# The state space's parameters of a hybrid trunk, moved from VectorE to GpSimd

## The chip, the core and the metric

The kernel runs on one core of a Trainium2 chip. Its engines are TensorE (PE, the matmuls; PEld is its weight load), VectorE (DVE), ScalarE (ACT), GpSimd (POOL) and SyncE (SP, which issues the DMAs here). Each engine works through its own instructions in a fixed order; semaphores hold an instruction back until its inputs are there. The metric is the device time of one execution in microseconds (us), less being better.

## What is computed

Two layers over a sequence of 256 positions with 2048 channels. The first ("even") layer projects its input by one wide matrix and feeds a state-space mixer and a gated MLP; the second ("odd") is a differential attention. The change touches only the mixer's parameters, which are small: 64 groups of 64 complex states, 4096 numbers, held as 128 partitions x 32.

```python
def s5_mixer(u, lam_re, lam_im, log_dt, b_re, b_im, c_re, c_im, d_skip):
    dt = jnp.exp(log_dt.astype(f32))[:, None]
    mag = jnp.exp(lr * dt)
    ab_re = mag * jnp.cos(li * dt)
    ab_im = mag * jnp.sin(li * dt)
    den = lr * lr + li * li
    nr = ab_re - 1.0
    f_re = (nr * lr + ab_im * li) / den
    f_im = (ab_im * lr - nr * li) / den
    ...
    _, _, h_re, h_im = lax.associative_scan(combine, (a_re, a_im, bu_re, bu_im), axis=1)
```

The kernel replaces the scan over positions by matmuls with tables of powers of the complex factor `ab`, and computes exp, sine and cosine itself from polynomials.

## The kernel before

**Weights.** The time goes into matmuls with fp32 weights that are streamed from memory in chunks of four 128-row tiles (two halves of 128x1024 each). Every weight is split in two: ACT makes a rounded copy `wh`, and DVE subtracts it to get the rest, `wl` (one DVE instruction of 128x1024 per half chunk, line 61). PE then makes three passes: `wh` by the high part of the activations (`hh`), `wl` by `hh`, and `wh` by their low part (`hl`). There are three buffers each for `wr` (raw), `wh` and `wl`, so DVE can be at most three half chunks ahead of PE. The activations' own low part `hl` is made by DVE in the first 25 us.

**Order of the chunks.** The first layer's projection runs as `v` (chunks 0 to 7), `xa` (8 to 15), `u` (16 to 23), then the gates, the output projection, and the odd layer. `xa` feeds the mixer, `u` and `v` the gated MLP. A chunk of `xa` is 48 matmuls. The main products share one PSUM pool of two buffers, so the first matmul of `u` needs the buffer that the first half of `xa` fills; it is free when DVE has read it out (`xs <- xa,rbc`).

**Side work.** Three generators run beside these matmuls. `ssm_params()` (line 386) computes, on arrays of 128x32, `dt` and `mag` (by `exact_exp`, line 358), sine and cosine (`ph`, `ph_s`, `ph_c`), `ab`, the reciprocal `den`, the factors `fc` and `fa`, and seven repeated squarings `pw[0]` to `pw[6]`. `e_tables(0)` (line 556) builds the table `E` from them: a copy of `pw[0]` into column 1 (line 563), then six steps k = 1 to 6, each of which multiplies the columns so far by `pw[k]` (eight products `em`, four sums into `E`) and so doubles the table. `ssm_consts()` (line 490) clears the blocks `bbr`, `cA`, `cN` on GpSimd, and builds the tables `m1fc`, `m2fc`, `m1fa`, `m2fa`, `m1ab`, `m2ab` on DVE, which ACT copies into `bbr` and `cA`; PE multiplies these (`pk`, 64 small matmuls, lines 532 and 533) and transposes them (`pbt`). GpSimd also scales an identity into `intra` (16 instructions of 128x128, line 482) and masks `bw` (line 657).

**What sets the order.** Each engine's order (but SP's) is fixed before the program runs, by a scheduler that simulates all engines and gives the earliest ready instruction its place. When one instruction's expected time changes, the order of the others on every engine can change with it.

**The helpers.** `tt`, `ts` and `stt` record two-input operations, operations with scalars, and `(a op s) op b`. Each fixes the engine for its line:

```python
    def tt(o, a, b, op, eng=None):
        (eng or V).tensor_tensor(out=o, in0=a, in1=b, op=op)
    def stt(o, a, s, b, op0, op1):
        V.scalar_tensor_tensor(out=o, in0=a, scalar=s, in1=b, op0=op0, op1=op1)
```

Of the kernel before, what the change touches and what calls it, by code (L numbers as in the profile page):

```python
# [10 lines left out]
F32 = mybir.dt.float32  # L11
# [18 lines left out]
def hybrid_trunk_kernel(ctx: ExitStack, tc: tile.TileContext, xT, xtok, w_in0, w_glu, w_out0,  # L30
                        w_in1, w_out1, pk, bc, lng, wsp, rope, subln, fnorm, out):
    nc = tc.nc
    V, A, PE, G, SP = nc.vector, nc.scalar, nc.tensor, nc.gpsimd, nc.sync
# [6 lines left out]
    sm = ctx.enter_context(tc.tile_pool(name="sm", bufs=1))  # L40
# [16 lines left out]
    def bcast(ap, shape):  # L57
        return ap.to_broadcast(shape)

    def tt(o, a, b, op, eng=None):  # L60
        (eng or V).tensor_tensor(out=o, in0=a, in1=b, op=op)  # L61

    def mul(o, a, b):
        tt(o, a, b, ALU.mult)

    def add(o, a, b):
        tt(o, a, b, ALU.add)

    def sub(o, a, b):
        tt(o, a, b, ALU.subtract)  # L70

    def ts(o, a, s1, op0, s2=None, op1=None):
        if op1 is None:
            V.tensor_scalar(out=o, in0=a, scalar1=s1, scalar2=None, op0=op0)
        else:
            V.tensor_scalar(out=o, in0=a, scalar1=s1, scalar2=s2, op0=op0, op1=op1)

    def stt(o, a, s, b, op0, op1):
        V.scalar_tensor_tensor(out=o, in0=a, scalar=s, in1=b, op0=op0, op1=op1)

    def act(o, i, f, **kw):
        A.activation(out=o, in_=i, func=f, **kw)  # L82
# [1 line left out]
    def rsqrt_mean(name, ss, n, eps, post=None):  # L84
# [6 lines left out]
        def v_y2(y):  # L91
            z = t("rq_z")
            if w == 1:
                stt(z, y, v, y, ALU.mult, ALU.mult)
            else:
                mul(z, y, y)
                mul(z, z, v)
            return z

        v = t("rq_v")  # L100
        ts(v, ss, 1.0 / n, ALU.mult, eps, ALU.add)
        g = t("rq_i", I32)
        ts(g, v.bitcast(I32), 1, ALU.logical_shift_right)
        ts(g, g, -1.0, ALU.mult, 1597463007.0, ALU.add)
        y = g.bitcast(F32)
        r = sm.tile([128, w], F32, name=name, tag=name, bufs=2)
        z = v_y2(y)
        u = t("rq_u")
        ts(u, z, 0.375, ALU.mult, -1.25, ALU.add)
        mul(u, u, z)  # L110
        stt(r, u, 1.875, y, ALU.add, ALU.mult)
        z = v_y2(r)
        c = 1.0 if post is None else post
# [84 lines left out]
    side = deque()  # L198
# [63 lines left out]
    def side1(name, shape, lane=0):  # L262
        return psb.tile(shape, F32, name=name, tag=f"sb{lane}")
# [45 lines left out]
    def h_split(k):  # L309
        hi = hh[k // 8][:, k % 8, :]  # L310
        with hp():
            act(hi, xt[:, k, :], AF.Copy, scale=g0[:, k:k + 1])
            stt(hl[k // 8][:, k % 8, :], xt[:, k, :], g0[:, k:k + 1], hi.bitcast(F32), ALU.mult, ALU.subtract)
# [39 lines left out]
    def tr32(name, shape=(128, 32), dt=F32):  # L353
        return sm.tile(list(shape), dt, name=name, tag=f"tr{shape[1]}{'i' if dt == I32 else ''}",
                       bufs=(7 if dt == F32 else 1) if shape[1] <= 32 else 2)

    def exact_exp(o, x, w=32):
        sh = (128, w)
        xc = tr32("e_x", sh)
        ts(xc, x, -104.0, ALU.max, 90.0, ALU.min)  # L360
        n = tr32("e_n", sh)
        ts(n, xc, 1.4426950408889634, ALU.mult)
        ts(n, n, MAGIC, ALU.add)
        ts(n, n, MAGIC, ALU.subtract)
        r = tr32("e_r", sh)
        stt(r, n, -0.693359375, xc, ALU.mult, ALU.add)
        stt(r, n, 2.12194440054690583e-4, r, ALU.mult, ALU.add)
        p = tr32("e_p", sh)
        ts(p, r, 1.0 / 5040, ALU.mult)
        for c in (1.0 / 720, 1.0 / 120, 1.0 / 24, 1.0 / 6, 0.5, 1.0):  # L370
            stt(p, p, c, r, ALU.add, ALU.mult)
        ts(p, p, 1.0, ALU.add)
        n1 = tr32("e_n1", sh)
        ts(n1, n, 0.5, ALU.mult)
        ts(n1, n1, MAGIC, ALU.add)
        ts(n1, n1, MAGIC, ALU.subtract)
        sub(n, n, n1)
        for part in (n1, n):
            e = tr32("e_i", sh, I32)
            ts(e, part, 127.0, ALU.add, 8388608.0, ALU.mult)  # L380
            mul(p, p, e.bitcast(F32))
        V.tensor_copy(out=o, in_=p)

    cst = {}

    def ssm_params():
        dt_ = p32("dt")
        exact_exp(dt_, log_dt)
        yield
        mag = p32("mag")  # L390
        z = tr32("lrdt")
        mul(z, lam_re, dt_)
        exact_exp(mag, z)
        r2 = p32("r2")
        mul(r2, mag, mag)
# [160 lines left out]
    def e_tables(half):  # L556
        E = big.tile([128, 2, 16, 128], F32, name=f"E{half}", tag="e")
        etab[half] = E
        hs = slice(half * 16, half * 16 + 16)
        pw = cst["pw"]  # L560
        V.memset(E[:, 0, :, 0:1], 1.0)
        V.memset(E[:, 1, :, 0:1], 0.0)
        V.tensor_copy(out=E[:, :, :, 1:2], in_=pw[0][:, :, hs].unsqueeze(3))
        for k in range(1, 7):
            n = 1 << k
            for q in range(2):
                ph = slice(q * 8, q * 8 + 8)
                es = E[:, :, ph, 0:n]
                sh = [128, 8, n]
                m = [t4(f"em{half}{k}{q}{i}", [128, 2, 8, 64])[:, :, :, 0:n] for i in range(2)]  # L570
                for i in range(2):
                    a = pw[k][:, i, half * 16 + q * 8:half * 16 + q * 8 + 8].unsqueeze(2).to_broadcast(sh)
                    for c in range(2):
                        mul(m[i][:, c], es[:, c], a)
                o = slice(n, 2 * n)
                sub(E[:, 0, ph, o], m[0][:, 0], m[1][:, 1])
                add(E[:, 1, ph, o], m[0][:, 1], m[1][:, 0])
            if k >= 4:
                yield
        yield  # L580
# [68 lines left out]
        for s in range(4):  # L649
            yield from ssm_set(half * 4 + s)  # L650

    side.append(ssm_params())
    side.append(e_tables(0))
    side.append(ssm_consts())

# [60 lines left out]
    for n in range(2):  # L716
# [4 lines left out]
        with hp():  # L721
            for t in range(2):
                act(ut[:, t, n * 512:(n + 1) * 512], ps[:, t, :], AF.Gelu_apprx_tanh, scale=rsx[0][:, t:t + 1])
                p = side1(f"s{n}{t}", [128, 4, 128])
# [3 lines left out]
                for g in range(4):  # L728
                    h = n * 4 + g
                    o = ut[:, t, h * 128:(h + 1) * 128]  # L730
                    stt(o, p[:, g, :], bspt[:, h:h + 1], o, ALU.add, ALU.mult)
    yh = {1: (t8(15, "yh1", [128, 8, T], F32R), t8(13, "yl1", [128, 8, T], F32R))}
    for n in range(2):
# [4 lines left out]
        with hp():  # L738
            for t in range(2):
                gt = t2(f"gt{n}{t}", [128, 512])  # L740
                act(gt, ps[:, t, :], AF.Silu, scale=rsx[0][:, t:t + 1])
                o = ut[:, t, n * 512:(n + 1) * 512]
                mul(o, o, gt)
            for c in range(2):
                c0 = n * 4 + 2 * c
                p = side1(f"ybT{c0}", [128, 2, T])
# [290 lines left out]
    for t in range(2):  # L1037
        s = slice(t * 128, (t + 1) * 128)
# [20 lines left out]
        for c in range(3):  # L1059
            o = x1[t][:, c * 512:(c + 1) * 512]  # L1060
# [96 lines left out]
```

## Time and profile before

| | before |
|---|---|
| time, median of 3 runs | 888.02 us (887.10 to 888.34) |
| the profiled execution | 886.45 us, of which its span 884.7 |
| PE busy | 866.4 us, 98% of the span |
| DVE busy | 680.2 us, 77% |
| ACT busy | 456.6 us, 52% |
| POOL busy | 36.8 us, 4%, in 55 instructions |

A reader takes the busy shares first (PE leaves 18 us of its span idle), then the stretches of the first 140 us, where the side work lies, and last the order and the start times of single instructions there. The durations that the trace gives for DVE are a little longer than the distance from one start to the next; where instructions follow each other without a gap, the distance is the cost.

### The profile page before, as it was taken

The page shows a single profiled execution, that of the slowest core. Times are in us where ns is not written, and L with a number is a line of the kernel's source. Part 1 is how long each engine was busy: PE and PEld are TensorE (multiplying, and loading weights), DVE is VectorE, ACT ScalarE, POOL GpSimd, SP SyncE. Part 2 cuts the span into 40 slices and gives each one's busy share as a digit, 9 for nine tenths or more (in the row PEclk, how much of TensorE's full clock was granted, in tenths as well). Part 3 has the DMA queues.
Part 4 walks back from the last instruction along what each step waited for, and adds up shares of the span by engine and source line. Part 5 has one row for each costly group of instructions (what it writes and reads, how often), then busy time and mean ns, then how long its engine had stood idle before and what let it go on. Part 6 is the DMA issues. An engine that isn't in the chain of part 4 may idle for free.

```text
span 884.7 us, 13127 instructions
## 1 busy us (share of the span) xinstructions
PE 866.4 (98%) x5086; PEld 749.2 (85%) x5086; DVE 680.2 (77%) x1267; ACT 456.6 (52%) x639; POOL 36.8 (4%) x55
## 2 busy tenths in 40 slices
PE   8999999999999999999999999999999999999995
PEld 6799978788999789888788888888888888888895
DVE  8999869999988766577876688667867687765773
ACT  7563862455334645565445544555446544554551
POOL 7100000000000100000000000000000000000000
PEclk9999999999999999999999999999999999999998
DMA  8965452234534655555554555555554555555542
GB/s 299 409 223 191 144 190 96 96 112 175 190 104 144 261 181 175 184 190 183 168 190 161 173 191 190 191 159 176 189 191 154 180 190 195 189 187 190 180 154 96
DMA packets 55167, 160.19 MB, mean 181 GB/s; under 512 B 3392, under 2 KB 37440, under 8 KB 41024
## 3 DMA queue, kind: packets, MB, share of 16 engines
q1 hardware_dynamic: 54528, 156.20, 50.4%
q0 software_dynamic: 576, 3.15, 0.9%
q8 instruction: 40, 0.66, 0.3%
q14 instruction: 23, 0.19, 0.1%
HBM read 157.24 MB, written 2.10 MB: 180 GB/s over the span
## 4 chain that ended last, share of the span: by engine, by line
PE 88%; DVE 7%; ACT 2%; issue 1%; DMA 1%; SPq 0%; DVEq 0%; ACTq 0%
PE k L249 7%; PE q L249 7%; PE v L223 4%; PE v L224 4%; PE v L222 4%; PE k L250 3%; PE q L250 3%; PE g L224 3%; PE g L223 3%; PE g L222 3%; PE od L223 2%; PE od L222 2%; PE od L224 2%; PE ga L235 2%; PE ga L238 2%; PE ga L237 2%
## 5 line engine op out<-in xcount | busy, mean ns | idle before, releaser
L82 ACT ACTIVATE wh<-wr 128x1024 fp32r<-128x1024 f32 (+1 forms) x276 | 288.7, 1047 | 347.5 <-PE v L224 59.6
L61 DVE TENSOR_TENSOR wl<-wr,wh 128x1024 fp32r<-128x1024 f32 (+1 forms) x276 | 332.2, 1206 | 131.1 <-ACT wh L82 130.0
L249 PE MATMUL k<-h2p,wh 128*128 128x512 f32 x256 | 90.7, 397 | 1.9 <-DVE rm L61 1.9
L249 PE MATMUL q<-h2p,wh 128*128 128x512 f32 x256 | 90.4, 396 | 0.0
L250 PE MATMUL q<-h2p,wl 128*128 128x256 f32 x256 | 72.3, 283 | 0.1
L250 PE MATMUL k<-h2p,wl 128*128 128x256 f32 x256 | 71.9, 282 | 0.0
L249 PEld LDWEIGHTS k<-h2p,wh 128*128 128x128 f32 x256 | 48.0, 188 | 13.3 <-DVE rm L61 2.2
L249 PEld LDWEIGHTS q<-h2p,wh 128*128 128x128 f32 x256 | 48.0, 188 | 10.8
L223 PE MATMUL v<-wl,h2p 128*128 128x512 f32 x128 | 50.8, 397 | 0.0
L223 PE MATMUL g<-wl,h2p 128*128 128x512 f32 x128 | 50.3, 393 | 0.0
L224 PE MATMUL g<-wh,h2p 128*128 128x512 f32 x128 | 50.1, 391 | 0.0
L224 PE MATMUL v<-wh,h2p 128*128 128x512 f32 x128 | 50.0, 391 | 0.0
L222 PE MATMUL g<-wh,h2p 128*128 128x512 f32 x128 | 49.9, 390 | 0.0
L222 PE MATMUL v<-wh,h2p 128*128 128x512 f32 x128 | 49.9, 390 | 0.0
L250 PEld LDWEIGHTS q<-h2p,wl 128*128 128x128 f32 x256 | 48.3, 189 | 0.6 <-DVE wl L61 0.4
L250 PEld LDWEIGHTS k<-h2p,wl 128*128 128x128 f32 x256 | 48.4, 189 | 0.1
L223 PE MATMUL od<-wl,oh 128*128 128x512 f32 x96 | 37.6, 392 | 0.0
L222 PE MATMUL od<-wh,oh 128*128 128x512 f32 x96 | 37.5, 391 | 0.0
L224 PE MATMUL od<-wh,ol 128*128 128x512 f32 x96 | 37.2, 390 | 0.0
L235 PE MATMUL ga<-hh,wh 128*128 128x256 f32 x128 | 36.6, 286 | 0.0
L238 PE MATMUL ga<-hh,wl 128*128 128x256 f32 x128 | 36.5, 286 | 0.0
L237 PE MATMUL ga<-hl,wh 128*128 128x256 f32 x128 | 36.4, 285 | 0.0
(329 smaller groups left out, 2057.7 us busy)
## 6 DMA issues: line engine op xcount, KB each, us to landing
wr<-in_w_in_dram SPq DMA_DIRECT2D x68, 1024.0 KB, 4.8
wr<-in_w_in_dram SPq DMA_DIRECT2D x68, 512.0 KB, 5.1
wr<-in_w_out_dram SPq DMA_DIRECT2D x32, 1024.0 KB, 4.8
wr<-in_w_glu_dram SPq DMA_DIRECT2D x4, 1024.0 KB, 4.8
wr<-in_w_in_dram SPq DMA_DIRECT2D x8, 256.0 KB, 4.8
xk<-in_xtok_dram SPq DMA_DIRECT2D x2, 1024.0 KB, 10.2
xr<-in_xtok_dram POOLq DMA_DIRECT2D x2, 1024.0 KB, 7.3
out_dram<-x SPq DMA_DIRECT2D x6, 256.0 KB, 2.5
```

The lines of the kernel that those rows point to most:

```text
L61: (eng or V).tensor_tensor(out=o, in0=a, in1=b, op=op)
L82: A.activation(out=o, in_=i, func=f, **kw)
L222: PE.matmul(ps[:, t, :], hi[:, s], wh, start=first and a == 0, stop=False)
L223: PE.matmul(ps[:, t, :], hi[:, s], wl, start=False, stop=False)
L224: PE.matmul(ps[:, t, :], lo[:, s], wh, start=False, stop=last and a == len(ktiles) - 1)
L235: PE.matmul(ps[:, c, :], wh[:, s], hi, start=first and a == 0 and c % 2 == 0, stop=False, skip_group_check=True)
L237: PE.matmul(ps[:, c, :], wh[:, s], lo, start=False, stop=False, skip_group_check=True)
L238: PE.matmul(ps[:, c, :], wl[:, s], hi, start=False, stop=fin, skip_group_check=True)
L249: PE.matmul(ps[:, c, :], wh[:, s], hl, start=first and a == 0, stop=False, skip_group_check=True)
L250: PE.matmul(ps[:, c, T:], wl[:, s], hl[:, 0], start=False, stop=a == len(ktiles) - 1 and not first, skip_group_check=True)
```

## The change

The three helpers no longer name VectorE but look up a list with one entry, `el`. A new wrapper `on_pool` sets the entry to GpSimd while the generator `ssm_params()` takes a step, and back to VectorE after it. [...]

```diff
+    el = [V]
+
     def tt(o, a, b, op, eng=None):
-        (eng or V).tensor_tensor(out=o, in0=a, in1=b, op=op)
+        (eng or el[0]).tensor_tensor(out=o, in0=a, in1=b, op=op)
...
     def stt(o, a, s, b, op0, op1):
-        V.scalar_tensor_tensor(out=o, in0=a, scalar=s, in1=b, op0=op0, op1=op1)
+        if el[0] is G:
+            n = o.shape[-1]
+            z = sm.tile([128, n], F32, name="gz", tag=f"gz{n}", bufs=1)
+            ts(z, a, s, op0)
+            tt(o, z, b, op1)
+        else:
+            V.scalar_tensor_tensor(out=o, in0=a, scalar=s, in1=b, op0=op0, op1=op1)
...
-        V.tensor_copy(out=o, in_=p)
+        el[0].tensor_copy(out=o, in_=p)
...
+    def on_pool(steps):
+
+        while True:
+            el[0] = G
+            try:
+                next(steps)
+            except StopIteration:
+                return
+            finally:
+                el[0] = V
+            yield
...
-    side.append(ssm_params())
+    side.append(on_pool(ssm_params()))
     side.append(e_tables(0))
     side.append(ssm_consts())
```

`ts` changes as `tt` does. The reciprocal of `den` stays on DVE, and so do the table `E` and the constants. In the program DVE has 136 instructions fewer (57 with two inputs, 38 with scalars, 39 `stt`, 2 copies), GpSimd 175 more (77 with scalars, 96 with two inputs, of which 15 are 128x64, and 2 copies); 145 of the 175 wait for an earlier result of GpSimd itself. ACT loads its function table twice more. PE and SP have the same instructions. Lines after the helpers stand 9 to 21 lines further down in the new file.

The order on three engines, at the places that matter. First DVE, around the copy that begins the table `E`, as it was (`pw_346` is `pw[0]`, `pw_355` is `pw[1]`, `E_449` the table; `rq` belongs to an rsqrt by integer steps):

```order
L61 TENSOR_TENSOR pw_346<-pw_346,pw_m 128x64
L61 TENSOR_TENSOR fc<-t_317,den 128x32
L61 TENSOR_TENSOR t_325<-nr,pkt 128x32
L76 TENSOR_SCALAR rq_v<-ss_177 128x2
L61 TENSOR_TENSOR pw_sq<-pw_346 128x64
L79 SCALAR_TENSOR_TENSOR pw_355<-pw_346 128x32
L61 TENSOR_TENSOR t_317<-ab,pkt 128x32
L563 COPY E_449<-pw_346 128x32
L74 TENSOR_SCALAR rq_i<-rq_v 128x2
L61 TENSOR_TENSOR pw_m<-pw_sq 128x32
```

The copy stands behind the last step of `pw[0]`, among the other small steps, which DVE works through between the `wl` of chunks 5 and 6. The same place in the changed program (`pw_410` is `pw[0]`; `wl_1_945` is the second half of chunk 7, `wl_0_975` and `wl_1_979` are chunk 8, then come chunks 9, 10 and the first half of 11):

```order
L64 TENSOR_TENSOR wl_1_945<-wr_125,wh_1_944 128x1024
L455 RECIPROCAL den<-den 128x32
L64 TENSOR_TENSOR wl_0_975<-wr_128,wh_0_974 128x1024
L64 TENSOR_TENSOR wl_1_979<-wr_128,wh_1_978 128x1024
...
L64 TENSOR_TENSOR wl_0_1116<-wr_938,wh_0_1115 128x1024
L64 TENSOR_TENSOR wl_1_1120<-wr_938,wh_1_1119 128x1024
L64 TENSOR_TENSOR wl_0_1174<-wr_972,wh_0_1173 128x1024
L64 TENSOR_TENSOR wl_1_1178<-wr_972,wh_1_1177 128x1024
L584 COPY E_527<-pw_410 128x32
L64 TENSOR_TENSOR wl_0_1232<-wr_1113,wh_0_1231 128x1024
L64 TENSOR_TENSOR em_531<-E_527,pw_421 128x8x2 x2
```

The small steps are gone, the reciprocal stands in front of the `wl` of `xa`'s first chunk, and the copy of `pw[0]` stands behind the `wl` of chunk 10 instead of between those of chunks 5 and 6. The 24 products and sums of k = 1 and 2 follow, with the second half of chunk 11, and then k = 3 in front of chunk 12 (`pw_443` is `pw[3]`):

```order
L64 TENSOR_TENSOR E_527<-em_555,em_556 128x8x4 x2
L64 TENSOR_TENSOR em_563<-E_527,pw_443 128x8x8
L64 TENSOR_TENSOR wl_0_1290<-wr_1171,wh_0_1289 128x1024
L64 TENSOR_TENSOR em_563<-E_527,pw_443 128x8x8
L64 TENSOR_TENSOR em_564<-E_527,pw_443 128x8x8 x2
L64 TENSOR_TENSOR em_571<-E_527,pw_443 128x8x8 x2
L64 TENSOR_TENSOR E_527<-em_563,em_564 128x8x8 x2
```

The first product of k = 3 now stands in front of the `wl` of chunk 12. From the copy to the first product of k = 3 there are two half chunks of `wl`; from there to the first product of k = 6 five; from there to `xs` six more, and 18 instructions of 128x512 that build the constants.

GpSimd's new work, where `pw[0]` is finished (`gz` is the scratch array, `pw_410` is `pw[0]`):

```order
L77 TENSOR_SCALAR gz<-ep 128x32
L77 TENSOR_SCALAR nr<-ab 128x32
L64 TENSOR_TENSOR t_389<-ab,pkt 128x32
L64 TENSOR_TENSOR pw_m<-pw_sq 128x32
L64 TENSOR_TENSOR pw_410<-pw_sq 128x32
L64 TENSOR_TENSOR pw_410<-gz,ep 128x32
L64 TENSOR_TENSOR t_381<-nr,pkt 128x32
L79 TENSOR_SCALAR pw_m<-pw_m 128x32
L64 TENSOR_TENSOR t_381<-t_381,t_389 128x32
L64 TENSOR_TENSOR pw_410<-pw_410,pw_m 128x64
L64 TENSOR_TENSOR fc<-t_381,den 128x32
```

Before, GpSimd had none of these rows. Of the new ones 122 come up to and with `pw[0]`'s last, 32 more to `pw[3]`'s, 21 more to `pw[6]`'s; the memsets of `cA` and `cN` and the masking of `bw` stand among the first 122.

PE, where the mixer's small products `pk` begin, as it was:

```order
L237 MATMUL xa_1476<-hl_155,wh_0_1537 128x256
L238 MATMUL xa_1476<-hh_153,wl_0_1538 128x256
L235 MATMUL xa_1476<-hh_153,wh_0_1537 128x256
L532 MATMUL pk_761<-cN,bbr_646 32x32
L237 MATMUL xa_1476<-hl_155,wh_0_1537 128x256
L238 MATMUL xa_1476<-hh_153,wl_0_1538 128x256
L235 MATMUL xa_1476<-hh_153,wh_0_1537 128x256
L237 MATMUL xa_1476<-hl_155,wh_0_1537 128x256
```

They stood inside `xa`'s matmuls, the first of them in chunk 14 of `xa`'s 8 to 15. In the changed program:

```order
L247 MATMUL xa_1554<-hh_153,wl_1_1678 128x256
L244 MATMUL xa_1554<-hh_153,wh_1_1677 128x256
L246 MATMUL xa_1554<-hl_155,wh_1_1677 128x256
L247 MATMUL xa_1554<-hh_153,wl_1_1678 128x256
L553 MATMUL pk_839<-cN,bbr_724 32x32
L554 MATMUL pk_839<-cN,bbr_726 32x32
L553 MATMUL pk_839<-cN,bbr_724 32x32
...
L553 MATMUL pk_839<-cN,bbr_724 32x32
L554 MATMUL pk_839<-cN,bbr_726 32x32
L569 MATMUL pbt_1070<-ident,bbr_724 128x128 x4
L231 MATMUL u_2096<-wh_0_1731,hh_152 128x512
```

All 64 of `pk` now stand behind the last matmul of `xa` and directly in front of `pbt` and `u`, so nothing of `xa` is left to run while `pk` waits for its inputs.

## Rows read from the trace of the kernel before

**Rows 1.** Stretches: length; busy us (instructions) of PE, PEld, DVE, ACT, POOL; clock, DMA, GB/s.

```profile
20.00:103.00 83.00, 82.42 (x666) 76.10 (x666) 81.35 (x262) 50.12 (x66) 4.79 (x3) 1.00 0.67 256
103.00:140.00 37.00, 35.00 (x175) 27.98 (x173) 26.21 (x51) 24.21 (x32) 0.00 (x0) 1.00 0.40 142
```

**Rows 2.** Waits of PE: what for; total us, times, longest.

```profile
PE v L223 <- DVE wl L61: 2.3, 3, 0.9
PE k L249 <- DVE rm L61: 1.9, 1, 1.9
```

**Rows 3.** Timeline of POOL: start, us, instruction [idle before <-releaser].

```profile
4.58 0.29 POOL masks.py:199 TENSOR_SCALAR_AFFINE_SELECT ident<-ident 128x128 f32<-128x128 f32 x1
4.97 13.35 POOL L482 TENSOR_SCALAR intra<-ident,pkt 128x128 f32<-128x128 f32 x16
33.71 1.82 POOL L496 MEMSET cA<- 128x2048 f32 x1 [15.39 <-ACT xsq L82]
36.55 1.81 POOL L497 MEMSET cN<- 128x2048 f32 x1 [1.03 <-ACT xsq L82]
47.64 1.16 POOL L657 TENSOR_SCALAR_AFFINE_SELECT bw<-bw 128x1024 f32<-128x1024 f32 x1 [9.28 <-DMA bw<-in_wsp_dram]
```

**Rows 4.** Groups of POOL, whole run: instruction, count | busy us, mean ns | idle before.

```profile
L1055 POOL TENSOR_TENSOR xf<-x,fn 128x256 f32<-128x256 f32 x4 | 2.9, 734 | 102.9 <-DVE x L61 102.9
```

**Rows 5.** The same view, 11 to 16.4 us (DVE busy throughout).

```profile
L482 POOL TENSOR_SCALAR intra<-ident,pkt 128x128 f32<-128x128 f32 x5 | 5.7, 1146 | 0.0
```

**Rows 6.** The same view, 17.74 to 18.35 us (DVE without work).

```profile
L482 POOL TENSOR_SCALAR intra<-ident,pkt 128x128 f32<-128x128 f32 x1 | 0.6, 600 | 0.0
```

**Rows 7.** Timeline of DVE.

```profile
33.12 0.18 DVE L79 SCALAR_TENSOR_TENSOR ph_c<-ph_c,ph_z 128x32 f32<-128x32 f32 x1
33.22 0.18 DVE L61 TENSOR_TENSOR den<-den,t 128x32 f32<-128x32 f32 x1
39.19 0.20 DVE L563 COPY E<-pw 128x32 f32<-128x32 f32 x1
...
88.06 1.22 DVE L61 TENSOR_TENSOR wl<-wr,wh 128x1024 fp32r<-128x1024 f32 x1
89.20 1.28 DVE L61 TENSOR_TENSOR m2fa<-bct,fa 128x512 f32<-128x512 f32 x2
90.40 0.68 DVE L61 TENSOR_TENSOR m2fc<-m2fc 128x512 f32<-128x512 f32 x1
101.42 1.23 DVE L61 TENSOR_TENSOR xs<-xa,rbc 128x1024 f32<-128x1024 f32 x1
```

**Rows 8.** Groups of DVE, 2 to 105 us.

```profile
L61 DVE TENSOR_TENSOR em<-E,pw 128x512 f32<-128x512 f32 x8 | 5.1, 682 | 0.0
L61 DVE TENSOR_TENSOR em<-E,pw 128x256 f32<-128x256 f32 x8 | 3.0, 413 | 0.0
L61 DVE TENSOR_TENSOR em<-E,pw 128x128 f32<-128x128 f32 x8 | 1.9, 278 | 0.0
L61 DVE TENSOR_TENSOR em<-E,pw 128x64 f32<-128x64 f32 x8 | 1.5, 218 | 0.0
L61 DVE TENSOR_TENSOR em<-E,pw 128x32 f32<-128x32 f32 x8 | 1.2, 181 | 0.0
L61 DVE TENSOR_TENSOR em<-E,pw 128x16 f32<-128x16 f32 x8 | 1.2, 166 | 0.0
L74 DVE TENSOR_SCALAR rbcp<-ones,rs 128x128 f32<-128x128 f32 x2 | 0.5, 276 | 0.0
```

**Rows 9.** Timeline of PE, at the first products of `xa` and of `u`.

```profile
53.69 0.28 PE L237 MATMUL xa<-hl,wh 128*128 128x256 f32 x1
53.81 0.28 PE L238 MATMUL xa<-hh,wl 128*128 128x256 f32 x1
...
103.10 0.48 PE L222 MATMUL u<-wh,hh 128*128 128x512 f32 x1
```

**Rows 10.** Groups of ACT, whole run.

```profile
L82 ACT ACT_TABLE_LOAD x15 | 19.2, 1283 | 1.1 <-PEq L1145 0.8
```

More of the change, by code (lines that the diff above doesn't have):

```diff
@@ L73, in ts @@
         if op1 is None:
-            V.tensor_scalar(out=o, in0=a, scalar1=s1, scalar2=None, op0=op0)
+            el[0].tensor_scalar(out=o, in0=a, scalar1=s1, scalar2=None, op0=op0)
         else:
-            V.tensor_scalar(out=o, in0=a, scalar1=s1, scalar2=s2, op0=op0, op1=op1)
+            el[0].tensor_scalar(out=o, in0=a, scalar1=s1, scalar2=s2, op0=op0, op1=op1)
     def stt(o, a, s, b, op0, op1):
-        V.scalar_tensor_tensor(out=o, in0=a, scalar=s, in1=b, op0=op0, op1=op1)
+        if el[0] is G:
[5 more added lines that the diff above has]
+            V.scalar_tensor_tensor(out=o, in0=a, scalar=s, in1=b, op0=op0, op1=op1)
     def act(o, i, f, **kw):
```

## The prediction, made before the changed kernel had run

> **What bounds the kernel now.** The busy shares come first: PE works 98% of the span, so only what makes PE wait, or lets it wait less, can move the time. The waits of PE say where it still waits: the longest single one is 1.9 us, in the odd layer, and the three on `wl` in `v` together are 2.3 us [rows 2]. Then the stretch in which the moved work lies. From 20 to 103 us DVE is busy 81.35 of 83 us, PE 82.42 and GpSimd only 4.79; from 103 to 140 us DVE is busy 26.21 of 37 and PE 35.00 [rows 1]. So DVE is full until `u` begins at 103.10 [rows 9] and loose behind it, and PE has at most about 2 us of idle time there in which a delay can be absorbed. A tempting reading is that taking work from a full DVE must help. But PE does not wait for DVE in that stretch (0.58 us idle in 83), since `wl` always stood in front of the small steps. The question is therefore not how much DVE sheds, but when the last thing that `u` needs is ready: the table `E` and the constants, then `xs`, all of them on DVE behind the `pw`.
>
> **What the change takes off DVE.** 136 instructions of mostly 128x32. They follow each other at 0.10 us [rows 7], so 13.6 us. None of it is on PE's path now, and by itself it shortens nothing but the 2.3 us of waits on `wl` and perhaps some tenths.
>
> **What one instruction costs on GpSimd.** The trace of before has none of 128x32, so its price is bounded. Two masks of 128 and 1024 columns take 0.29 and 1.16 us [rows 3]: 0.97 ns a column and a fixed 0.164 us. The product of 128x256 takes 0.734 us [rows 4]; less that fixed part it is 2.2 ns a column, so 32 columns cost 0.235 us. The scaling of 128 columns takes 0.600 us while DVE has no work [rows 6], by the same way 3.4 ns a column and 0.27 us for 32. Over 77 with scalars and 98 others the mean is 0.25 us. 145 of the 175 also wait for a result of GpSimd itself; the hand-over between the mask of the identity and the scaling behind it, 4.58 + 0.29 to 4.97, is 0.10 us [rows 3], so with a rounded 0.09 another 0.075 us on the mean. That makes 0.33 us with DVE quiet. With DVE busy on two-input work the same scaling takes 1.146 us instead of 0.600 [rows 5, 6], and the 16 of them on the mean 13.35 / 16 = 0.834 [rows 3], 1.39 times the quiet one. In that stretch the two-input work of DVE filled some two thirds of the time; from 20 to 54 us of the changed order I reckon 16 halves of `wl` at 1.14 [rows 7] and a little `hl`, three fifths, so I take 1.35 times: 0.25 x 1.35 + 0.075 = **0.415 us**. The lower end is 0.30 (a fixed price below that of the mask, little loss to DVE). The upper one is 0.60: if the 0.600 of the scaling is all fixed price, the mean is (77 x 0.600 + 98 x 0.235) / 175 = 0.40, by 1.35 and with the hand-over 0.61. I take the middle since a price by columns is what the two masks show.
>
> **When the `pw` are ready.** GpSimd ends `intra` at 4.97 + 13.35 = 18.32 [rows 3]. Then come the memsets of `cA` and `cN` and the mask, 1.82 + 1.81 + 1.16 = 4.8 us [rows 3], and 122 new instructions up to `pw[0]`: 23.1 + 122 x 0.415 = 73.7 us. `pw[3]` is 32 later, 87.0; `pw[6]` 21 more, 95.7. On the way `den` is ready after 82 of them, 18.3 + 3.6 + 82 x 0.415 = 55.9 us. DVE's reciprocal waits for it in front of the `wl` of `xa`'s first chunk, which PE wants at 53.8 [rows 9]: PE loses some 3 us there, which the later wait swallows.
>
> **What stands behind the `pw`.** The copy into `E` ran at 39.19 [rows 7]. Now it stands behind the `wl` of chunk 10. A chunk of `xa` is 48 matmuls 0.12 us apart [rows 9], 5.75 us, and DVE can be three halves ahead, so that `wl` can't be ready before 53.5 + 3 x 2.87 + ACT's copy and its own 2.2 = 64.4 us, however fast GpSimd is. From the copy the order of DVE is fixed. Each step k is 12 instructions at the group's mean less 0.08 (recorded means of 0.68 us stand for starts 0.60 apart) [rows 7, 8]: k = 1 and 2 1.0 and 1.2 us, k = 3 to 5 1.7 + 2.4 + 4.0 = 8.0, k = 6 7.2. To the first product of k = 3 there are two `wl`, so it can begin at 64.4 + 2.3 + 2.2 = 69.0 at best; by the price above it begins at 87.0, when `pw[3]` is there. From it to k = 6 are 8.0 us and five `wl` at 1.14: 13.7. From there to the end of `xs` are six `wl` (6.8), 7.2, eighteen of 128x512 at 0.60 (10.8), `xs` itself with the short steps around it (1.5), and half a us of idle, as DVE had 1.65 in 83 [rows 1]: some 27.0. So `xs` ends at 87.0 + 13.7 + 27.0 = 127.7 us, and `u` begins then instead of at 103.10: **24.6 us late**. PE's order gives no cover: `pk` stands behind all of `xa`, and PE waits at k = 3, at `pk` and at `u`. Of this PE can give back the 2.0 us that it idles from 103 to 140 [rows 1], since the weights behind it are then there. Nothing later has more idle time that the delay could fill.
>
> ACT's two further table loads of 1.28 us [rows 10] lie where ACT is half idle (50.12 of 83) [rows 1] and cost nothing; without that cover they would cost 2.6.
>
> The sum: 886.45 + 24.6 - 2.0 = 909.1 us on the profiled execution. The median of the runs is 1.57 higher, so 910.6.
>
> By general form, with x the price of one instruction, `u` begins at 63.8 + 154 x, and not before 109.7: 1.5 us for each hundredth of x.
>
> **Where the Trainium skill speaks against it.** GpSimd's scaling of 128x128 took 0.600 us with DVE quiet [rows 6], DVE's own of that size 0.276 [rows 8]. The Trainium skill, "GPSIMD Engine Reference", section "4.1 Engine selection", has GpSimd about 2 times slower than DVE for two inputs and at about the line rate for one; for one input this trace disagrees. By that rule the mean would be near 0.15 plus the hand-over, and the time would be that of the first rival. In the other direction, the same instruction took 1.146 us beside a busy DVE [rows 5]. The Trainium skill, "SBUF — State Buffer", section "Who interferes with whom", says that a DVE instruction with two SBUF inputs and a GpSimd instruction that reads SBUF share a port pair, held by one as an exclusive lock; if each `wl` shut GpSimd out for its whole length, 16 of 1.14 would add 18 us to 122 x 0.33 and give about the same time, some 6 us more than mine.
>
> The granted clock was 1.00 in both stretches [rows 1], and PE never waited over 1.9 us at once [rows 2], so the trace does not show what a wait of ten does. The Trainium skill, "TensorE: Matmul & The Clock Gate", Part 1, says that an idle array drops to 1.2 GHz and starts again at that rate: by it a few us more, which stand in neither sum.
>
> **The rivals.** First, *GpSimd keeps up and only the new order costs*: at x up to 0.34 the start of `u` is between 109.7 and 116.2 us, 6.6 to 13.1 late, less 2.0, so 892.6 to 899. For it speak the short width and the quiet price of 0.33; against it the 1.39 times beside DVE. Second, *each instruction has a fixed price of half a us or more*: x over 0.51 puts `u` at 142 us and more, 925 to 940. For it speaks 1.146 us beside a busy DVE; against it the masks' price by columns. Third, on the other side, *DVE's relief wins*: the 13.6 us that DVE sheds remove PE's 2.3 us of waits on `wl`, and the time falls to 885.7. It decides if `u` can begin by 103.1, that is if k = 3 began by 62.4; the order lets it begin at 69.0 at best, since the copy stands behind chunk 10. It could only come true if `wl` ran further ahead than three buffers allow, or if `xs` did not hold `u`. Last, that nothing moves: the order shows all 175 on GpSimd, so this needs the same relief and delay to cancel.
>
> **How the numbers follow.** GpSimd late, x of 0.34 to 0.51, 899 to 925, around 910.6: 0.60. GpSimd keeps up, 892.6 to 899: 0.18. Fixed price, 925 to 940: 0.16. DVE's relief: 0.03. No change: 0.03. The range takes the first two and the lower edge of the third: 893 to 927, which leaves out about 0.16. A measurement of this kernel can tell some 0.2% from no change. Faster by more than that: 0.03; within it: 0.03; slower: 0.94.
>
> **What would show it.** Right: GpSimd's new instructions start some 0.4 us apart; the copy into `E` at about 74 us; DVE idle, waiting for GpSimd, before it and before k = 3; PE waiting a few us at `xa`'s first chunk and for ten or more in front of `pk` and `u`; `u` beginning near 128 us; and everything behind `u` as before, shifted by some 22 us. Wrong: a spacing on GpSimd far from 0.4 us (then 1.5 us for each hundredth); `wl` and the products of DVE longer than 1.14 and 0.60 apart because GpSimd holds them up, which this sum has at nothing; or a later part that does not shift with `u`.

## The result: 913.73 us, 3% slower

The changed kernel takes 913.73 us (median of 4 runs, 912.65 to 915.70) against 887.56 us of the kernel before in the same runs: a ratio of 1.0298, 95% interval 1.0284 to 1.0312, so 26.2 us longer. Forecast were 910.6 us, range 893 to 927, and slower with a chance of 0.94. The profiled execution has a span of 912.5 us, 27.8 longer than the one before.

The stretches of the trace that answer to [rows 1], in the same columns (length; busy us of PE, PEld, DVE, ACT, POOL; clock, DMA, GB/s):

```profile
20.00:40.00 20.00, 20.00 (x89) 16.52 (x88) 13.45 (x26) 13.86 (x17) 17.34 (x37) 1.00 1.02 419
40.00:60.00 20.00, 13.15 (x60) 10.51 (x58) 5.05 (x9) 11.70 (x19) 17.44 (x48) 0.95 0.54 216
60.00:80.00 20.00, 19.43 (x146) 19.44 (x147) 8.54 (x12) 5.69 (x6) 17.97 (x45) 0.88 0.46 158
80.00:103.00 23.00, 20.57 (x155) 19.97 (x154) 20.59 (x66) 7.01 (x7) 16.02 (x49) 0.93 0.37 138
103.00:130.00 27.00, 15.51 (x218) 14.52 (x216) 26.33 (x42) 12.28 (x17) 0.00 (x0) 0.75 0.33 117
130.00:167.00 37.00, 34.47 (x171) 27.81 (x172) 24.54 (x46) 23.94 (x33) 0.00 (x0) 1.00 0.32 114
```

DVE, busy 81.35 of the 83 us before `u`, now works 13.45, 5.05 and 8.54 of three times 20 us, while GpSimd is busy 17 to 18 in each. From 80 us on DVE is full again. PE loses 6.9 us between 40 and 60 and 11.5 between 103 and 130. Behind that, from 130 to 167, it looks as from 103 to 140 before.

GpSimd's timeline, which answers to [rows 3] (start, us, instruction):

```profile
9.93 9.94 POOL L503 TENSOR_SCALAR intra<-ident,pkt 128x128 f32<-128x128 f32 x11
19.96 1.65 POOL L77 TENSOR_SCALAR e_n<-e_n 128x32 f32<-128x32 f32 x2
...
45.58 1.82 POOL L517 MEMSET cA<- 128x2048 f32 x1
...
59.34 1.31 POOL L77 TENSOR_SCALAR gz<-ph_s 128x32 f32<-128x32 f32 x1
60.74 1.03 POOL L64 TENSOR_TENSOR ph_s<-gz,ph_z 128x32 f32<-128x32 f32 x1
61.85 0.29 POOL L77 TENSOR_SCALAR gz<-ph_s 128x32 f32<-128x32 f32 x1
62.22 1.33 POOL L64 TENSOR_TENSOR ph_s<-gz,ph_z 128x32 f32<-128x32 f32 x1
...
77.66 0.32 POOL L64 TENSOR_TENSOR pw<-pw,pw_m 128x64 f32<-128x64 f32 x1
...
87.19 0.32 POOL L64 TENSOR_TENSOR pw<-pw,pw_m 128x64 f32<-128x64 f32 x1
```

The chain begins at 19.96, finishes `pw[0]` at 77.66 + 0.32 = 77.98 and `pw[3]` at 87.51. Most instructions take 0.25 or 0.29 us, the others 1.0 to 1.3. The long ones stand where DVE makes a `wl`. DVE's timeline, which answers to [rows 7], shows this and what waits for the chain (in brackets the idle time before an instruction, and what ended it):

```profile
46.15 1.23 DVE L64 TENSOR_TENSOR wl<-wr,wh 128x1024 fp32r<-128x1024 f32 x1 [2.48 <-ACT wh L91]
59.08 0.35 DVE L455 RECIPROCAL den<-den 128x32 f32<-128x32 f32 x1 [11.71 <-POOL den L64]
59.35 2.30 DVE L64 TENSOR_TENSOR wl<-wr,wh 128x1024 fp32r<-128x1024 f32 x2
...
62.22 1.22 DVE L64 TENSOR_TENSOR wl<-wr,wh 128x1024 fp32r<-128x1024 f32 x1
...
78.02 0.24 DVE L584 COPY E<-pw 128x32 f32<-128x32 f32 x1 [4.71 <-POOL pw L64]
...
81.67 0.96 DVE L64 TENSOR_TENSOR em<-E,pw 128x16 f32<-128x16 f32 x6 [2.19 <-POOL pw L64]
...
85.64 0.91 DVE L64 TENSOR_TENSOR em<-E,pw 128x32 f32<-128x32 f32 x6 [0.60 <-POOL pw L64]
...
87.59 0.21 DVE L64 TENSOR_TENSOR em<-E,pw 128x64 f32<-128x64 f32 x1
...
129.38 1.23 DVE L64 TENSOR_TENSOR xs<-xa,rbc 128x1024 f32<-128x1024 f32 x1 [0.37 <-ACT cA L91]
```

The two `wl` from 59.35 to 61.65 lie over GpSimd's long instructions at 59.34 and 60.74, the `wl` at 62.22 over that of 62.22. DVE stands still 11.71 us for `den`, 4.71 for `pw[0]`, 2.19 for `pw[1]` and 0.60 for `pw[2]`, and begins k = 3 (the first `em` of 128x64) at 87.59, 0.08 us behind `pw[3]`. In front of k = 3 itself it does not wait: the work of k = 2 ends just as `pw[3]` comes. The `xs` that `u` needs ends at 130.61.

PE's waits, as [rows 2], and its first matmul of `u`, as [rows 9]:

```profile
PE xa L247 <- DVE wl L64: 8.2, 2, 5.9
PE pk L553 <- issue: 5.5, 1, 5.5
PE pk L554 <- ACT bbr L91: 5.0, 1, 5.0
...
PE xa L244 <- ACT wh L91: 1.5, 1, 1.5
```

```profile
130.75 0.47 PE L231 MATMUL u<-wh,hh 128*128 128x512 f32 x1 [1.69 <-DVE rq_u L79]
```

`u` begins at 130.75, 27.65 us later than at 103.10. (Where the view says `issue`, it names no releaser; `rq_u` is a small step of DVE that ends just behind `xs`.) The waits in front of `pk` and `u` are those that the order of PE made possible: nothing of `xa` is left to run there.

### The profile page after: what moved, and what is told of

Its sections match the earlier page's. It is cut to its first block, busy times and chain, and to the rows that moved or that the text cites. A ratio compares the mean times of both kernels' runs of the same rounds, so it can differ in the third digit from the quotient of the medians.

```text
span 912.5 us, 13169 instructions
## 1 busy us (share of the span) xinstructions
PE 874.8 (96%) x5086; PEld 755.9 (83%) x5086; DVE 667.9 (73%) x1131; ACT 460.4 (50%) x641; POOL 102.3 (11%) x230
## 4 chain that ended last, share of the span: by engine, by line
PE 82%; POOL 8%; DVE 5%; issue 2%; ACT 2%; DVEq 0%; POOLq 0%; ACTq 0%
PE k L258 7%; PE q L258 6%; PE k L259 3%; PE q L259 3%; PE v L232 3%; PE g L233 3%; PE v L233 3%; PE g L232 3%; PE g L231 3%; PE v L231 3%; PE od L231 2%; PE od L232 2%; PE od L233 2%; PE W L616 2%; POOL gz L77 2%
## 5 line engine op out<-in xcount | busy, mean ns | idle before, releaser
L910 POOL MEMSET rm<- 32x512 f32 x16 | 8.2, 518 | 394.2 <-DVE qkT L64 313.4
L247 PE MATMUL xa<-hh,wl 128*128 128x256 f32 x128 | 38.7, 302 | 8.4 <-DVE wl L64 8.2
L244 PE MATMUL xa<-hh,wh 128*128 128x256 f32 x128 | 37.8, 295 | 1.5 <-ACT wh L91 1.5
L246 PE MATMUL xa<-hl,wh 128*128 128x256 f32 x128 | 37.7, 294 | 0.0
```

Of the source, the lines that this page charges most:

```text
L244: PE.matmul(ps[:, c, :], wh[:, s], hi, start=first and a == 0 and c % 2 == 0, stop=False, skip_group_check=True)
L246: PE.matmul(ps[:, c, :], wh[:, s], lo, start=False, stop=False, skip_group_check=True)
L247: PE.matmul(ps[:, c, :], wl[:, s], hi, start=False, stop=fin, skip_group_check=True)
```

## Experiments

The theory was the forecast's: GpSimd delivers late; DVE, held in a fixed order, waits; and `u` begins late by that. Its rivals: the new order does it, whoever computes the parameters; GpSimd's traffic slows DVE; PE's lost time at `xa` adds up; or any use of GpSimd costs the same. Times stand beside 887.4 to 887.9 us of the kernel before in the same runs.

### What an instruction costs, and what DVE does to it

To the kernel before a measuring tail is added behind its last output: chained pairs of a scaling and a sum on GpSimd, alone and beside DVE.

```diff
+    def chain(n, w):
+        p, g, c = P[:, 0:w], P[:, 256:256 + w], P[:, 512:512 + w]
+        for _ in range(n):
+            G.tensor_scalar(out=g, in0=p, scalar1=0.5, scalar2=None, op0=ALU.mult)
+            G.tensor_tensor(out=p, in0=g, in1=c, op=ALU.add)
+    chain(8, 32)
+    chain(4, 128)
...
+    chain(16, 32)
+    for _ in range(14):
+        tt(R, Q, R, ALU.min)
...
+    chain(16, 32)
+    for _ in range(24):
+        ts(Q, Q, 0.5, ALU.mult)
```

> The kernel before with a measuring tail behind its last output: chained pairs of a scaling and a sum on GpSimd, 8 of 128x32, 4 of 128x128, 8 of 128x32 with DVE idle; 16 pairs of 128x32 beside 14 two-input DVE instructions of 128x1024; 16 pairs with DVE idle; 16 pairs beside 24 one-input DVE instructions of 128x1024. Its whole time is not compared. Theory (price by columns, and an exclusive hold of a shared port): quiet pair of 128x32 0.65 to 0.75 us from start to start, of 128x128 0.9 to 1.3; beside two-input DVE at least 1.3 per pair, with single instructions of 1.0 us and more; beside one-input DVE as quiet. Rival (fixed price): 128x128 costs no more than 128x32. Rival (no hold, only a share): beside two-input DVE every instruction longer by the same share, none over 0.6.

GpSimd's timeline: a pair of 32 columns alone, and the scalings with which two pairs in a row begin, for 128 columns alone, for 32 beside DVE's two-input instructions, and for 32 beside its one-input ones.

```profile
882.49 0.29 POOL L1077 TENSOR_SCALAR bn<-bn 128x32 f32<-128x32 f32 x1 [5.44 <-DVE bn L1072]
882.86 0.25 POOL L1078 TENSOR_TENSOR bn<-bn 128x32 f32<-128x32 f32 x1
883.20 0.29 POOL L1077 TENSOR_SCALAR bn<-bn 128x32 f32<-128x32 f32 x1
...
888.16 0.53 POOL L1077 TENSOR_SCALAR bn<-bn 128x128 f32<-128x128 f32 x1
...
889.32 0.53 POOL L1077 TENSOR_SCALAR bn<-bn 128x128 f32<-128x128 f32 x1
...
900.03 1.21 POOL L1077 TENSOR_SCALAR bn<-bn 128x32 f32<-128x32 f32 x1
...
902.55 1.21 POOL L1077 TENSOR_SCALAR bn<-bn 128x32 f32<-128x32 f32 x1
...
936.95 0.68 POOL L1077 TENSOR_SCALAR bn<-bn 128x32 f32<-128x32 f32 x1
...
938.41 0.68 POOL L1077 TENSOR_SCALAR bn<-bn 128x32 f32<-128x32 f32 x1
```

DVE's in the same tail (15 and 24 instructions in a row each):

```profile
898.38 17.83 DVE L61 TENSOR_TENSOR bn<-bn,bn 128x32 f32<-128x32 f32 x15 [16.07 <-POOL bn L1078]
...
935.34 17.44 DVE L74 TENSOR_SCALAR bn<-bn 128x1024 f32<-128x1024 f32 x24 [0.36 <-POOL bn L1091]
```

Alone a pair is 0.71 us from start to start (882.49 to 883.20), so 0.354 for a chained instruction of 32 columns; of 128 columns it is 1.16. So the price has a fixed part and a part by columns, as the prediction had it. Beside two-input work a pair is 2.52 us: each GpSimd instruction now takes as long as one of DVE's 128x1024, and the two engines take turns: DVE's 15 instructions, of which one is small, take 17.83 us, so about 1.26 each instead of the 1.14 of [rows 7]. The expectation for one-input work was wrong: there a pair takes 1.46, each GpSimd instruction again as long as one of DVE's, and DVE itself 17.44 / 24 = 0.73 us. So either form of DVE's large instructions shuts GpSimd out for its whole length. These lengths are from one execution. The Trainium skill, "SBUF — State Buffer", section "Who interferes with whom", says just this of two-input instructions and, for a one-input one, only of its two-port modes; this trace agrees with the first. The second would account for the one-input row, but no run here shows in which mode DVE worked. What the Trainium skill, "GPSIMD Engine Reference", section "4.1 Engine selection", says, that GpSimd runs one-input work at about line rate, did not hold here: a chained scaling of 32 columns took 0.37 us (882.49 to 882.86), more than the sum's 0.34.

### GpSimd busy, but nobody waiting for it

The kernel before, with a chain as long as the new one, on scratch data.

```diff
+        G.tensor_scalar(out=z, in0=log_dt, scalar1=0.01, scalar2=None, op0=ALU.mult)
+        for i in range(87):
+            G.tensor_scalar(out=y, in0=z, scalar1=0.5, scalar2=None, op0=ALU.mult)
+            G.tensor_tensor(out=z, in0=y, in1=log_dt, op=ALU.add)
...
     side.append(ssm_params())
```

> The kernel before, with 175 extra GpSimd instructions of 128x32 (one scaling, then 87 pairs of scaling and sum, each waiting for the one before) on scratch data that nobody reads. Theory (GpSimd's lateness is what costs; its running beside DVE is free for the others): time within 0.3% of before, 887 to 890 us; a pair takes about 0.8 us on the mean from 19 us on (0.4 each), with single instructions of 1.0 to 1.3 us beside a long subtraction of DVE. Rival (GpSimd's traffic slows DVE's two-input work, and so PE): PE waits on wl grow by several us, 893 us or more, and DVE's wl and em are longer than 1.22 and 0.68 us.

Measured: 891.01 us, ratio 1.0039 (1.0026 to 1.0053), 3.6 us longer. The groups of GpSimd from 18 to 100 us and of DVE from 2 to 125 us:

```profile
L657 POOL TENSOR_SCALAR spy<-spz 128x32 f32<-128x32 f32 x63 | 34.8, 552 | 5.5
L658 POOL TENSOR_TENSOR spz<-spy,pkt 128x32 f32<-128x32 f32 x63 | 31.7, 503 | 4.9
```

```profile
L61 DVE TENSOR_TENSOR em<-E,pw 128x256 f32<-128x256 f32 x8 | 4.0, 538 | 0.0
```

GpSimd's instructions took 0.55 and 0.50 us beside a DVE that is full, and a pair with the idle time before it some 1.2 us, where 0.8 was expected. DVE pays too: the products of 256 columns take 538 ns on the mean instead of 413 [rows 8], and `u` begins at 107.7. The time is just above the band of the theory and below that of the rival: beside a full DVE, GpSimd's presence costs a few us, though nobody waits for it. A part may come from the order, in which the memsets of `cA` and `cN` moved 9 and 10 us later; that was not separated. The 3.6 us are not a share of the 26.2: in the changed kernel DVE stands still for 33 of the 60 us from 20 to 80. None of it was in the sum.

### The order without GpSimd

The kernel before, all on DVE, with the first column of `E` made to depend on the `wl` of chunk 10, and table and constants recorded there.

```diff
-        V.memset(E[:, 0, :, 0:1], 1.0)
+        if half:
+            V.memset(E[:, 0, :, 0:1], 1.0)
+        else:
+            late = halves[10][3][1][:, 0:16].unsqueeze(2).bitcast(F32)
+            V.tensor_scalar(out=E[:, 0, :, 0:1], in0=late, scalar1=0.0, scalar2=1.0, op0=ALU.mult, op1=ALU.add)
...
-    side.append(e_tables(0))
-    side.append(ssm_consts())
...
+            if half == 0 and k == 2:
+                side.append(e_tables(0))
+                side.append(ssm_consts())
+                run_side(1000)
...
```

> The kernel before, all parameters on DVE, but the table E (its first column) and the constants are made to depend on wl of chunk 10's second half, so that the first steps of E and all behind them stand where the changed kernel has them. No GpSimd work added. The order also brings the normalisation of v (four instructions of 128x1024 on DVE, 4.6 us) into this stretch. Theory (the place behind chunk 10 is a floor that costs by itself): u begins at 110 to 119 us, time 895 to 903. Rival (the order is free, all is GpSimd's price): u by 105 us, 889 us or less. If it is 912 or more, the order alone explains the change.

Measured: 902.88 us, ratio 1.0179 (1.0151 to 1.0207), `u` at 114.9. It is inside its band but tells little: the scheduler brought the normalisation of `v` forward too, and another 5 us were lost inside `u`. A second version keeps that normalisation behind the constants:

> As the run with the late table, but with the normalisation of v kept behind the table and the constants, as in the changed kernel. All parameters on DVE, no work for GpSimd added; E's first column depends on wl of chunk 10's second half. Theory (the place behind chunk 10 is a floor: first product of k = 3 at about 69 us, 43 us from there to the end of xs): u begins at 109 to 113 us, time 893 to 897. Rival (the order is free): u by 105, 889 or less. Rival (the order explains nearly all): u past 122, 906 or more.

Measured: 897.35 us, ratio 1.0110 (1.0097 to 1.0124), 9.5 us longer, `u` at 114.2, both a little above the theory's band and well below the rival's that the order explains nearly all. DVE's timeline at the column, the first product of k = 3 and `xs`:

```profile
64.82 0.18 DVE L565 TENSOR_SCALAR E<-wl 128x16 f32<-128x16 f32 x1
...
70.68 0.63 DVE L61 TENSOR_TENSOR em<-E,pw 128x64 f32<-128x64 f32 x4
...
112.79 1.22 DVE L61 TENSOR_TENSOR xs<-xa,rbc 128x1024 f32<-128x1024 f32 x1 [0.37 <-ACT cA L82]
```

The column is written at 64.82 (the floor was put at 64.4), k = 3 begins at 70.68 (69.0), and from there to the end of `xs` are 43.3 us. In the changed kernel they are 43.0, from 87.59 to 130.61, with the same eleven `wl`. PE's order is alike too: here it waits 2.4 and 5.2 us in front of `pk` and 1.7 in front of `u`. So the two differ by when k = 3 begins, 16.9 us, and the times by 26.2 - 9.5 = 16.7 us. This splits the change, to a us or so: **9.5 us are the place behind chunk 10, which the scheduler chose, and 16.7 us are GpSimd being later than that place.**

### The same chain, started earlier

The changed kernel, with `intra` made to need `pw[6]`, so that GpSimd does it last.

```diff
+        zq = sm.tile([128, 16], F32, name="zq")
+        G.tensor_scalar(out=zq, in0=cst["pw"][6][:, 0, 0:16], scalar1=0.0, scalar2=None, op0=ALU.mult)
+        G.tensor_tensor(out=zq, in0=zq, in1=dq, op=ALU.add)
...
-            G.tensor_scalar(out=intra[:, i, :], in0=ident, scalar1=dq[:, i:i + 1], scalar2=None, op0=ALU.mult)
+            G.tensor_scalar(out=intra[:, i, :], in0=ident, scalar1=zq[:, i:i + 1], scalar2=None, op0=ALU.mult)
```

> The changed kernel, with the 16 scalings of an identity on GpSimd (13.4 us) put behind the parameters instead of in front of them. GpSimd's chain starts some 15 us earlier. Theory (pw[3] on GpSimd sets when k = 3, and so u, begins): pw[3] at about 74 us instead of 87.5, u at 118 to 121 instead of 130.8, time 900 to 905. Rival (something else sets u, such as PE's lost time at xa or the order): 911 to 915.

Measured: 907.69 us, ratio 1.0229 (1.0212 to 1.0246), `u` at 125.1. GpSimd's timeline at `pw[3]` and at `intra`:

```profile
73.80 1.17 POOL L64 TENSOR_TENSOR pw<-pw,pw_m 128x64 f32<-128x64 f32 x1
...
85.97 14.25 POOL L506 TENSOR_SCALAR intra<-ident,zq 128x128 f32<-128x128 f32 x10
```

`pw[3]` came at 74.97, as expected, and the time fell by 6 us, so the chain's lateness is on the path. But it fell by less than expected. The order changed with it. DVE begins k = 3 only at 77.14, 10.4 us earlier than in the changed kernel; k = 3 stands three `wl` earlier, so 14 of them instead of 11 lie between it and the end of `xs`, and that stretch takes 47.9 us instead of 43.0. `intra` now runs beside the table `E`, too: four products of 512 columns take 2.67 us there instead of 2.49. GpSimd's work was moved from where DVE idles to where DVE is the path.

### PE's lost time at `xa`

The changed kernel, with `den` and its reciprocal computed first.

```diff
+        den = p32("den")
+        t0 = p32("t0")
+        mul(den, lam_re, lam_re)
+        mul(t0, lam_im, lam_im)
+        add(den, den, t0)
+        V.reciprocal(out=den, in_=den)
         dt_ = p32("dt")
         exact_exp(dt_, log_dt)
...
-        mul(den, lam_re, lam_re)
-        mul(t1, lam_im, lam_im)
-        add(den, den, t1)
-        V.reciprocal(out=den, in_=den)
```

> The changed kernel, with den and its reciprocal computed first of all, before the first exponential, so that DVE no longer stops for it in front of xa's first chunk (11.7 us of DVE, 7.4 us of PE). Theory (that loss is swallowed by the later wait for pw): 912 to 915 us as the changed kernel, PE's 5.9 us wait at xa gone and found again later. Rival (it adds up): 905 to 908.

Measured: 915.05 us (914.68 to 915.20), ratio 1.0313 (1.0298 to 1.0329), `u` at 132.1. DVE's timeline at the copy:

```profile
79.77 0.23 DVE L585 COPY E<-pw 128x32 f32<-128x32 f32 x1 [9.43 <-POOL pw L64]
```

DVE no longer stops 11.71 us for `den`; it waits 9.43 us for `pw[0]` instead of 4.71. PE waits 2.65 us at `xa`'s first chunk instead of 7.42, and 4.35 us at a later one (81.33) instead of 2.30. The chain itself was 1.3 us later, with `pw[3]` at 88.84, and `u` and the time moved by just that. The rival, 905 to 908, is out: what PE loses at `xa` is swallowed by the wait for the powers.

### Less of it on GpSimd

The changed kernel, with only the first n steps of `ssm_params()` on GpSimd: the exponential `dt` (n = 1), both exponentials (2), sine and cosine too (3).

```diff
+        left = [n]
         while True:
-            el[0] = G
+            el[0] = G if left[0] > 0 else V
+            left[0] -= 1
```

> The changed kernel, with only the first exponential (dt) on GpSimd, ready at about 36 us instead of 17. Theory: the powers come some 10 us later than before, u begins 2 to 6 us late, time 888 to 893. Rival (any use of GpSimd costs the same): 913. Rival (relief of DVE wins once little is late): below 887.

> The changed kernel, with only the two exponentials (dt and mag) on GpSimd. mag is ready at about 55 us and DVE's order has the copy into E behind it. Theory: k = 3 at about 64, u at 112 to 115, time 894 to 899. Rival (any use of GpSimd costs the same): 913.

> The changed kernel, with only the first three steps on GpSimd (both exponentials, sine and cosine); ab, fc, fa and the powers on DVE as before. Theory (dose by what GpSimd still delivers late): ep is ready at about 75 us as in the changed kernel, the powers follow within some us on DVE, k = 3 at about 82, u at 125, time 905 to 911. Rival (any use of GpSimd costs the same, by the order): 913.

| on GpSimd | time, us | ratio (interval) | copy into `E` | `u` begins |
|---|---|---|---|---|
| nothing | 887.9 | 1 | 39.2 | 103.1 |
| `dt` | 895.45 | 1.0081 (1.0064 to 1.0098) | 53.0 | 112.5 |
| `dt`, `mag` | 896.86 | 1.0102 (1.0086 to 1.0118) | 56.3 | 114.7 |
| with sine and cosine | 911.29 | 1.0267 (1.0248 to 1.0285) | 78.0 | 130.1 |
| all | 913.73 | 1.0298 (1.0284 to 1.0312) | 78.0 | 130.8 |

DVE's timelines, where it first needs GpSimd's result: the first exponential's, then `mag`, then `ep`.

```profile
34.17 0.19 DVE L64 TENSOR_TENSOR lrdt<-pkt,dt 128x32 f32<-128x32 f32 x1 [3.21 <-POOL dt L391]
```

```profile
52.20 0.22 DVE L64 TENSOR_TENSOR ab<-ep,mag 128x64 f32<-128x64 f32 x1 [0.62 <-POOL mag L391]
```

```profile
73.98 0.23 DVE L64 TENSOR_TENSOR ab<-ep,mag 128x64 f32<-128x64 f32 x1 [7.92 <-POOL ep L64]
```

The cost grows with the time of the copy (though the last two rows, with the same time, lie 2.4 us apart), so it is not true that any use of GpSimd costs the same. The second and third are in or within 0.3 us of their bands. The first is 2.5 us above its band: `dt` came at 34 us, but all that DVE had done between 17 and 34 us before now had to be done behind it, and DVE had nothing else to do meanwhile. From the start to `u` DVE is idle 3.47 + 1.65 = 5.1 us in the kernel before and 8.6 + 6.7 = 15.3 here; the 10.2 us more are the 9.4 us by which `u` is late and 0.8 us of work that DVE sheds.

### Work on GpSimd that nothing waits for early

The kernel before, with only the fourteen steps of `fc` and `fa` on GpSimd, which feed the constants and not the powers.

```diff
+        el[0] = G
         mul(t1, nr, lam_re)
...
+        el[0] = V
         cst.update(ab=ab, fc=fc, fa=fa, ep=ep)
...
-    side.append(on_pool(ssm_params()))
+    side.append(ssm_params())
```

> The kernel before, with only the fourteen steps of fc and fa moved to GpSimd: they feed the constants (wanted on DVE from about 80 us) and not the powers, and DVE sheds fourteen instructions, 1.4 us. Theory (PE waits for nothing on DVE in this stretch, so relief of DVE is worth nothing, and what is wanted late costs nothing): within 0.2% of before, 886.0 to 889.5. Rival (relief of DVE pays): 1 us or more faster, 886 or less. Rival (any use of GpSimd holds DVE up): 890 or more.

Measured: 889.80 us (12 runs, 888.15 to 892.65), ratio 1.0029 (1.0017 to 1.0040), 1.9 us longer; 0.3 us outside the band. The memset of `cN` on GpSimd moved two us later with it. GpSimd's, DVE's and PE's timelines there:

```profile
38.63 1.81 POOL L520 MEMSET cN<- 128x2048 f32 x1
```

```profile
38.49 1.97 DVE L79 TENSOR_SCALAR rq_v<-ss 128x2 f32<-128x2 f32 x1
```

```profile
44.14 0.79 PE L232 MATMUL v<-wl,hh 128*128 128x512 f32 x1 [2.70 <-DVE wl L64]
```

A scalar instruction of two columns takes 1.97 us beside the memset; the `wl` behind it is late, and PE waits 2.70 us for it. In all PE waits 4.3 us for `wl` in `v`, against 2.3 [rows 2]. So the relief of DVE bought nothing. That this one hold makes the 1.9 us fits these waits, but was not tested.

## Why the prediction was right, and which terms were off

**The mechanism** held at all but one of the steps that it named: DVE idle in front of the copy into `E`, PE waiting at `xa`, `pk` and `u`, and everything behind `u` shifted as a whole. DVE's wait in front of k = 3 was not there: its last waits were for `pw[1]` and `pw[2]`, and `pw[3]` came as k = 2 ended. The relief of DVE was worth nothing, as forecast; where little else came with it (`fc` and `fa`), the time did not fall.

**The price of an instruction** was put at 0.415 us. From 19.96 to 77.98, less 1.82 and 1.81 for the memsets and 2.14 for the mask of `bw`, are 52.2 us for 120 instructions: 0.435. From there to `pw[3]` 32 took 9.53 us: 0.298. All together 0.406. The quiet price was right in size (0.33 forecast, 0.354 measured when chained, 0.21 to 0.28 where no result is awaited). Wrong was the form of what DVE adds: not 1.35 times on each, but nothing on most and a whole instruction of DVE on some. That rule stood in the prediction as the Trainium skill's ("SBUF — State Buffer", "Who interferes with whom"), at 16 turns of 1.14 us and a result 6 us above the forecast. The trace bears the rule out, but of 122 instructions fifteen were held, by some 0.9 us each, about 14 us, since DVE stood still for most of the time from 46 to 78. The factor of 1.35 gave about the same sum by another way; that is luck.

**When the powers came**: `pw[0]` at 77.98 instead of 73.7, since `intra` ended 1.5 us later than reckoned (it shared GpSimd with the chain's first steps), the mask took 2.14 instead of 1.16, and the price was a little higher up to there; `pw[3]` at 87.51 instead of 87.0. The last is partly luck: dearer up to `pw[0]`, cheaper behind it, where most instructions wait for no earlier result.

**From k = 3 to the end of `xs`** the sum said 40.7 us; it took 43.0. The stretch in the changed kernel, in the columns of the windows:

```profile
87.59:130.61 43.02, 30.79 (x336) 29.40 (x335) 42.28 (x85) 18.18 (x24) 8.67 (x21) 0.83 0.37 137
```

DVE idles 0.74 us there, about as reckoned (0.5), so its work was under-counted, by some 2 us of 42.28. Two parts are seen. Four short steps that each need the one before, and a wait for ACT, stand in front of `xs`: from the first of them to the end of `xs` it took 130.61 - 128.22 = 2.4 us, where the sum had 1.5 for all. And GpSimd still works 8.67 us beside the first steps, which makes products and `wl` longer; the prediction had this at nothing and named it as a sign of being wrong. The group of the products of 128 columns in the changed kernel:

```profile
L64 DVE TENSOR_TENSOR em<-E,pw 128x128 f32<-128x128 f32 x8 | 2.3, 332 | 0.0
```

They take 332 ns on the mean instead of 278 [rows 8], those of 64 columns 244 instead of 218, those of 256 columns 429 instead of 413: 0.8 us over the 24 of them. In the run of the order alone the stretch has no work on GpSimd:

```profile
70.68:114.01 43.33, 34.20 (x377) 33.45 (x375) 41.07 (x82) 20.29 (x26) 0.00 (x0) 0.88 0.41 146
```

There DVE works 1.2 us less and idles 2.3 us, 1.5 of it waiting for `wh` of ACT, so the likeness of 43.0 and 43.3 is partly chance, by a us or so. This is the term that was mis-sized most: of the 3.0 us by which `u` began later than forecast it makes 2.3, and `pw[3]` 0.5.

**`den`** was ready at 59.05 instead of 55.9, and PE lost 7.4 us instead of 3 at `xa`. This cost nothing, as the run with `den` first shows.

**What PE gives back** was put at 2.0 us. `u` begins 27.65 us late and its last matmul is 25.9 late (195.8 against 169.9), the second layer's first matmul 26.4 (429.5 against 403.1). So PE gave back 1.8. In this execution another 1.4 us were lost later, in the second layer; the medians differ by 26.2, and that the 1.4 us belong to the change is not shown.

**The rivals.** That only the order costs would have been 892.6 to 899; the run of the order alone gave 897.35, so the rival's number was right and its condition, a price up to 0.34 us, was missed by 0.07. The fixed price of half a us is out: 128 columns cost 1.16 us a pair and 32 cost 0.71. DVE's relief is out.

## What to carry to other kernels

A full engine is not a reason to take work from it: look whether the bound engine waits for it, and what the work that is moved releases. Work that heads a chain, moved to an engine on which each step costs three times as much or more (here 0.35 us against 0.10), leaves the first engine idle early and full late; the loss is the idle time, not the price. For such a chain on GpSimd these runs suggest reckoning each small instruction at its quiet price, and adding up to one whole large DVE instruction (here 0.9 us of 1.14) for each that DVE starts meanwhile; and count what GpSimd does to DVE in return, at the place where DVE is the path.

## What the runs showed of the hardware

GpSimd and DVE shut each other out by whole instructions: beside 128x1024 work of DVE a chained GpSimd instruction of 32 columns takes 1.26 us (two inputs on DVE) or 0.73 (one input) instead of 0.354. GpSimd's memsets behave otherwise: the one of `cA` at 45.58 took its 1.82 us under the `wl` at 46.15, which took its 1.23. But in the run with `fc` and `fa` the memset of `cN` held a small one-input instruction of DVE for 1.97 us.

In the long wait before `u` the granted clock fell. The stretches of the changed kernel there (columns as above):

```profile
120.00:125.00 5.00, 0.61 (x23) 0.61 (x25) 4.87 (x10) 1.89 (x3) 0.00 (x0) 0.50 0.02 5
125.00:130.00 5.00, 4.06 (x116) 3.60 (x111) 4.46 (x11) 4.89 (x8) 0.00 (x0) 0.54 0.00 0
```

From 120 to 125 us PE works 0.61 us of 5 and the clock is 0.50 of full speed, the lower of the two levels (1.2 of 2.4 GHz). In the next 5 us PE works 4.06 us on `pk` and `pbt` and the clock is 0.54 on the mean, so mostly still at the lower level. From 130 us on, where `u` begins, it is 1.00. The Trainium skill, "TensorE: Matmul & The Clock Gate", Part 1, says that an idle array drops to 1.2 GHz; this trace agrees. The slow matmuls had time: behind them PE waits another 1.69 us for DVE before `u`, and DVE, which idles 0.74 us from 87.59 to 130.61, did not wait for PE. So the few us that the prediction named for this are not seen in the start of `u`; no run tested the clock by itself.
